# A gated linear recurrence in a decoder trunk: score products of two heads in one run, 64-column levels, later start of the head pairs

## The chip, the cores and the metric

One core of one Trainium2 chip runs the kernel. The metric is the device time of one execution in microseconds (us), as the median of several runs. TensorE (PE; PEld is its weight load) multiplies matrices, VectorE (DVE) and ScalarE (ACT) work element by element, GpSimd (POOL) and SyncE (SP) issue most of the transfers.

## What is computed

Two layers of a decoder trunk on 256 tokens of width 2048, all in float32. Layer 0 mixes tokens with a gated MLP (mixer A) and a gated linear recurrence with 8 heads of width 128 (mixer B), layer 1 with a forgetting attention; each layer ends with a gated MLP. The part that the change touches is mixer B:

```python
def hgrn2(q, f_logit, i, g, lower_bound, o_gain):
    ...
    log_f = jnp.logaddexp(jnp.log(lb), jnp.log1p(-lb) + jax.nn.log_sigmoid(fl))
    k = (1.0 - lb) * jax.nn.sigmoid(-fl)
    ...
    def step(state, xs):
        q_c, k_c, v_c, lf_c = xs
        G = jnp.cumsum(lf_c, axis=2)
        o_inter = jnp.einsum('bhtk,bhkv->bhtv', q_c * jnp.exp(G), state)
        diff = G[:, :, :, None, :] - G[:, :, None, :, :]
        decay = jnp.exp(jnp.where(mask[:, :, None], diff, -jnp.inf))
        scores = jnp.einsum('bhtk,bhtsk,bhsk->bhts', q_c, decay, k_c)
        o_intra = jnp.einsum('bhts,bhsv->bhtv', scores, v_c)
        ...
    o = rms_norm(o, o_gain) * jax.nn.silu(g.astype(f32).reshape(shp))
```

## The kernel before

The weights stream through the core once, and nearly all of TensorE's work is their products. A float32 weight tile w is split into two rounded halves: ScalarE writes wh (L212), VectorE the remainder wl = w - wh (L217), and three matmuls (wh with the high part of the activations, wl with the high part, wh with the low part) stand for one in full precision: L273 to L275 in project_tok, L293 to L295 in project_four. One call of weights() loads 128x1024 numbers into one of four buffers w; wh and wl have three buffers each. The 12 matmuls that use one such tile are called a step below; a projection to 512 columns has 8 steps.

Small work is fitted between the steps by generators. At each step tick() runs every generator in `free` and `flight` up to its next yield; `after(n, g)` starts one n ticks later; `depth[0]` limits how many taken from `queue` are in flight. The helpers behind(), act_in(), mm_in() and others (L150 to L168) fix where an instruction stands in its engine's queue: behind the last conversion, subtraction or weight matmul that was handed over. So the order on every engine is fixed when the program is built, and each engine works through its queue in that order; a wait holds everything behind it on the same engine.

In mixer_ab the projections run in the order w_v, then for j = 0, 1 w_f, w_q and w_i (gates, queries and values of four heads each), then w_u and w_g, and the output projection w_abo. queries(j) starts the heads: `after((4, 3)[j] * i + 1 - i // 2, hgrn(4 * j + i))`. hgrn(h) replaces the decay between tokens of 128 by products on seven levels (blocks of 64, 32, ... 1 tokens):

- Factors of keys and queries are scaled level by level on VectorE (L621 to L628) and copied by ScalarE into E (L617), which has two buffers.
- TensorE forms the product between the two halves of the sequence (from t, called kq in the profile, into a bank px) and two products of 64x64 for each level into the two banks `level` (levels in the profile): four levels in the first, three in the second, each 128 columns wide. For the first level the products lie off the diagonal blocks, for the others on them; the columns that no product writes were set to zero once (L430).
- VectorE masks each bank (L646) into smk and adds the seven levels one by one to st[:, 1] (L651), which was set to the diagonal before (L605). st has three buffers.
- Three yields later st[:, 1] is transposed on TensorE (L168), copied back by ScalarE (L658), and three products with the values itok give the output (px<-itok). Then follow the norm (two squares L669, rsq(), two scalings L673).

`finish`, `values` and `mixes` prepare mixer A; `of_queries` reads the query sums z once and sums into dgc (L702). gated(j) multiplies the gate of w_g into itok (zg, L720) and transposes it (L313). spatial(j) waits until all heads have ended, then takes a Gelu of w_u's result (turn) and splits eight blocks into ya, one block each second tick. Switching between function sets costs a table load on ScalarE (L97).

Of the kernel before, what the change touches and what calls it, by code (L numbers as in the profile page):

```python
# [15 lines left out]
P = 128  # L16
S = 256
# [18 lines left out]
LANE = 64  # L36
LEVELS = (64, 32, 16, 8, 4, 2, 1)
# [18 lines left out]
def tile_trunk(ctx: ExitStack, tc: tile.TileContext, x, pp_d, cst_d, mlev_d, msk_d,  # L56
# [367 lines left out]
    def mixer_ab(norm):  # L424
# [4 lines left out]
        for b in level:  # L429
            V.memset(b, 0.0)  # L430
# [54 lines left out]
        msk = hp.tile([P, NL * P], BF16, tag="msk", name="msk")  # L485
# [5 lines left out]
        def values():  # L491
            behind(V.tensor_copy(msk, kst), "sub")
# [103 lines left out]
        depth[0] = 3  # L596

        itoks, left = [], [NH]

        def hgrn(h):  # L600
# [32 lines left out]
            smk = hp.tile([P, NL * P], F32, tag="smk", name=nm("smk"), bufs=1)  # L633
            xps = bank()
            mm_in(xps[:, 0:P], t[:, 0], t[:, 1], start=True, stop=True)
            s128 = hp.tile([P, P], F32, tag="s128", name=nm("s128"), bufs=3)
            SC.activation(s128, xps[:, 0:P], AF.Copy)
            for c0, c1 in ((0, 4), (4, NL)):
                sps = level[c0 // 4]
                for li in range(c0, c1):  # L640
                    for g in range(2):
                        k0 = g * (P // 2)
                        q0 = P // 2 - k0 if li == 0 else k0
                        mm_in(sps[k0:k0 + P // 2, (li - c0) * P + q0:(li - c0) * P + q0 + P // 2],
                              E[:, li, 0, k0:k0 + P // 2], E[:, li, 1, q0:q0 + P // 2], start=True, stop=True)
                V.tensor_tensor(smk[:, c0 * P:c1 * P], sps[:, 0:(c1 - c0) * P],  # L646
                                msk[:, c0 * P:c1 * P], ALU.mult)
                for li in range(c0, c1):
                    n = LEVELS[li]
                    sv = view(st[:, 1], 0, (2 * n, 64 // n), (n - P, 2), (1, n))  # L650
                    V.tensor_tensor(sv, sv, smk[:, li * P:(li + 1) * P].rearrange(  # L651
                        "p (b two n) -> p b two n", two=2, n=n), ALU.add)
# [5 lines left out]
            SC.activation(st[:, 1], op[:, S:S + P], AF.Copy)  # L658
# [6 lines left out]
            PE.matmul(op[:, P:S], s128, i0, start=True, stop=False)  # L665
            PE.matmul(op[:, P:S], st[:, 1], i1, start=False, stop=True)
# [71 lines left out]
        def spatial(j, z):  # L738
            while left[0] or j and yB[4 * j - 1] is None:
                yield  # L740
            yield
            act_in(z, z, AF.Gelu)
            yield
            for i in range(4):
                b = 4 * j + i
                m = mg[b].rearrange("p (t n) -> p t n", t=2)
                sum_in(m, m, natural(z[:, i]), ALU.mult)
                yB[b] = quad("ya")
                split(yB[b], mg[b], turn=True)
                yield  # L750
                yield
# [480 lines left out]
```

## Time and profile before

| | us |
|---|---|
| median of 3 runs | 2286.31 |
| lowest and highest run | 2285.83, 2288.68 |
| profiled execution, its time | 2286.77 |
| profiled execution, span from first to last instruction | 2284.7 |
| granted TensorE clock, mean | 1.000 |
| of the span, TensorE busy | 2279.6 |
| VectorE busy | 1561.6 |
| ScalarE busy | 1312.6 |

How to read the rows: in a timeline a row is start, duration, engine, line, operation, output<-inputs, shapes and count, and in brackets how long the engine had been idle before it and what ended that. In the list of groups a row ends with the count, then busy us and the mean ns of one, then the idle time before. In the list of waits a row says who waited for whom: us in total, how many times, the longest. A float32 matmul leaves two records, one of the rounded form leaves one; matmuls overlap, so the distance between two starts, not the duration, is what one takes from TensorE.

### The profile page before, as it was taken

The numbers are of one execution on the slowest core, as the hardware profiler recorded it, in microseconds if no ns is written. First come the engines' busy times: TensorE is split into PE (matmuls) and PEld (weight loads), VectorE is DVE, ScalarE is ACT, GpSimd is POOL, SyncE is SP. The second block draws the span as 40 slices with busy tenths as digits, with TensorE's granted clock in tenths as the row PEclk, the third lists the DMA queues.
The fourth block names the chain that finished last, engine by engine and source line by source line (L and its number), as shares of the span: only waits on it lengthen the run. The fifth ranks groups of instructions, "written<-read, shape, count | busy, mean of one in ns | idle before, by whom it ended". The sixth has DMA issues, their size and how long they took to land. (4 is left out here: it accounts for less than half of the span.)

```text
span 2284.7 us, 31585 instructions
## 1 busy us (share of the span) xinstructions
PE 2279.6 (100%) x10486; PEld 1895.7 (83%) x10486; DVE 1561.6 (68%) x2378; ACT 1312.6 (57%) x1957; POOL 420.3 (18%) x779
## 2 busy tenths in 40 slices
PE   9999999999999999999999999999999999999999
PEld 8888888888888888888888888888888888888887
DVE  7888767767467657766775665667776466667766
ACT  7577756656456445554555556655665455455642
POOL 0212232221012002201322211322311012012102
PEclk9999999999999999999999999999999999999999
DMA  8756677777667667766676656677777667666765
GB/s 283 216 178 188 199 217 218 242 222 216 201 195 234 207 201 218 214 214 183 186 226 210 197 176 196 206 225 240 224 218 217 195 209 219 207 210 211 223 204 175
DMA packets 487908, 481.06 MB, mean 211 GB/s; under 512 B 102880, under 2 KB 454640, under 8 KB 487744
## 3 DMA queue, kind: packets, MB, share of 16 engines
q1 hardware_dynamic: 460080, 448.42, 63.6%
q0 software_dynamic: 25360, 27.37, 5.0%
q10 hardware_dynamic: 2304, 3.26, 0.4%
q8 instruction: 82, 1.34, 0.2%
q14 instruction: 82, 0.67, 0.1%
HBM read 434.85 MB, written 2.12 MB: 191 GB/s over the span
## 5 line engine op out<-in xcount | busy, mean ns | idle before, releaser
L217 DVE TENSOR_TENSOR wl<-w,wh 128x1024 fp32r<-128x1024 f32 (+1 forms) x814 | 987.2, 1216 | 632.3 <-ACT wh L212 622.3
L212 ACT ACTIVATE wh<-w 128x1024 fp32r<-128x1024 f32 (+1 forms) x814 | 854.6, 1052 | 779.5 <-PE pm L295 566.1
L293 PE MATMUL pm<-wh,a 128*128 128x512 f32 x1792 | 700.8, 391 | 0.0
L295 PE MATMUL pm<-wh,a 128*128 128x512 f32 x1792 | 698.1, 390 | 0.0
L294 PE MATMUL pm<-wl,a 128*128 128x512 f32 x1792 | 697.8, 389 | 0.0
L319 POOL DMA_DIRECT2D zt<-tmp x413 | 223.6, 549 | 1197.4 <-DVE tmp L313 1050.8
L295 PEld LDWEIGHTS pm<-wh,a 128*128 128x128 f32 x1792 | 336.5, 188 | 70.0
L293 PEld LDWEIGHTS pm<-wh,a 128*128 128x128 f32 x1792 | 336.6, 188 | 69.7
L294 PEld LDWEIGHTS pm<-wl,a 128*128 128x128 f32 x1792 | 336.6, 188 | 69.1
L319 POOL DMA_DIRECT2D turn<-tmp x336 | 182.0, 550 | 543.6 <-DVE tmp L313 314.0
L293 PE MATMUL pm<-wh,hid 128*128 128x512 f32 x688 | 267.9, 389 | 0.0
L294 PE MATMUL pm<-wl,hid 128*128 128x512 f32 x688 | 267.9, 389 | 0.0
L295 PE MATMUL pm<-wh,hid 128*128 128x512 f32 x688 | 267.8, 389 | 0.0
L273 PE MATMUL pm<-wh,a 128*128 128x512 f32 x456 | 181.0, 397 | 0.0
L274 PE MATMUL pm<-wl,a 128*128 128x512 f32 x456 | 178.0, 390 | 0.2 <-DVE wl L217 0.2
L275 PE MATMUL pm<-wh,a 128*128 128x512 f32 x456 | 177.9, 390 | 0.0
L293 PEld LDWEIGHTS pm<-wh,hid 128*128 128x128 f32 x688 | 129.2, 188 | 26.8
L294 PEld LDWEIGHTS pm<-wl,hid 128*128 128x128 f32 x688 | 129.2, 188 | 26.7
L295 PEld LDWEIGHTS pm<-wh,hid 128*128 128x128 f32 x688 | 129.2, 188 | 26.7
L313 DVE STREAM_TRANSPOSE tmp<-z 128x512 f32<-128x512 f32 x132 | 91.9, 705 | 20.2 <-ACT z L1008 18.7
L159 ACT ACTIVATE conv<-zt,pp 128x256 f32<-128x256 f32 x176 | 95.3, 589 | 14.4 <-DMA zt<-tmp 9.4
L274 PEld LDWEIGHTS pm<-wl,a 128*128 128x128 f32 x456 | 85.8, 188 | 17.9 <-DVE wl L217 0.9
(225 smaller groups left out, 1925.6 us busy)
## 6 DMA issues: line engine op xcount, KB each, us to landing
w<-in_w_up SPq DMA_DIRECT2D x352, 512.0 KB, 4.5
w<-in_w_dn SPq DMA_DIRECT2D x176, 512.0 KB, 4.5
w<-in_w_cqkv SPq DMA_DIRECT2D x88, 512.0 KB, 4.3
w<-in_w_abo SPq DMA_DIRECT2D x32, 512.0 KB, 4.4
w<-in_w_cg SPq DMA_DIRECT2D x32, 512.0 KB, 3.9
w<-in_w_co SPq DMA_DIRECT2D x32, 512.0 KB, 4.9
zt<-tmp SPq DMA_DIRECT2D x414, 32.0 KB, 2.5
zt<-tmp POOLq DMA_DIRECT2D x413, 32.0 KB, 2.5
```

The costliest lines, as they stand in the source:

```text
L159: return behind(SC.activation(*args, **kw), "act")
L212: deep["act"] = SC.activation(wh[:, p], w[:, p], AF.Copy)
L217: deep["sub"] = V.tensor_tensor(wl[:, p], w[:, p], wh[:, p].bitcast(F32), ALU.subtract)
L273: PE.matmul(ps[T], ah, h, start=k + i == 0, stop=False)
L274: PE.matmul(ps[T], ah, l, start=False, stop=False)
L275: deep["main"] = PE.matmul(ps[T], al, h, start=False, stop=k + i == KT - 1)
L293: PE.matmul(ps[T], ah, h, start=k + i == 0, stop=False)
L294: PE.matmul(ps[T], ah, l, start=False, stop=False)
L295: deep["mm"] = deep["main"] = PE.matmul(ps[T], al, h, start=False, stop=k + i == n - 1)
L313: V.transpose(tmp.rearrange("p (b m i t) -> p b m i t", b=4, m=4, t=2)[:, :, :, :, T], src(T).rearrange("p (m b j) -> p b m j", m=4, b=4))
L319: qs[(a + b) % len(qs)].dma_start(dst[BLK * b:BLK * (b + 1), :, a * n:(a + 1) * n], tmp[BLK * a:BLK * (a + 1), b * 4 * n:(b + 1) * 4 * n] ...
```

## The change

Four things are changed, all in mixer_ab.

- One run for two heads. The even head of a pair waits until the odd head's factors E are made, and issues the products of both: two kq products into one bank, then 14 level products of the even head and 14 of the odd one. The bank level[i] now holds all seven levels of one head, 64 columns each.
- Masking and adding. The first level is copied by ScalarE straight into its off-diagonal place in st (two copies of 64x64). The other six are multiplied with a mask of 384 columns by one instruction, summed by one reduction over the levels, multiplied with tri (which puts the sum into the two halves of the rows), and added with the diagonal piece dg by two instructions of 64 partitions.
- Score tiles are four fixed tiles sts, cleared once; the transposed scores go to s128[:, 1] instead of back into st. The masks tri and eye are made once in values(), which has two yields more.
- Times. START gives new starts for the heads (before: 1, 5, 8, 12 and 1, 4, 6, 9 ticks; now 1, 4, 11, 14 and 1, 3, 8, 10), depth[0] is 4 instead of 3, and spatial() yields twice only after every second block.

```diff
+HP = P // 2
+START = ((1, 4, 12, 15), (1, 3, 9, 11))
...
-        for b in level:
-            V.memset(b, 0.0)
...
-        msk = hp.tile([P, NL * P], BF16, tag="msk", name="msk")
+        msk = hp.tile([P, NL - 1, HP], BF16, tag="msk", name="msk")
+        tri = hp.tile([P, 2, HP], F32, tag="tri", name="tri")
+        eye = hp.tile([P, HP], F32, tag="eye", name="eye")
+        sts = [hp.tile([P, 2, P], F32, tag=f"st{i}", name=f"st{i}") for i in range(4)]
...
         def values():
-            behind(V.tensor_copy(msk, kst), "sub")
+            full = kst.rearrange("p (l c) -> p l c", l=NL)
+            for g in range(2):
+                k = slice(g * HP, (g + 1) * HP)
+                behind(V.tensor_copy(msk[k], full[k, 1:, k]), "sub")
+            sum_in(eye, ident[:, 0:HP], ident[:, HP:P], ALU.add)
+            yield
+            behind(V.memset(tri, 0.0), "sub")
+            for li in range(1, NL):
+                n = LEVELS[li]
+                part = view(tri[:, 1], 0, (2 * n, 32 // n), (n - HP, 2), (1, n))
+                V.tensor_tensor(part, part, msk[:, li - 1].rearrange("p (b two n) -> p b two n", two=2, n=n), ALU.add)
+            yield
+            for st in sts:
+                behind(V.memset(st, 0.0), "sub")
             yield
...
-        depth[0] = 3
+        depth[0] = 4
...
-            st = hp.tile([P, 2, P], F32, tag="st", name=nm("st"), bufs=3)
-            V.tensor_tensor(st, ident.unsqueeze(1).to_broadcast([P, 2, P]),
-                            dgc[:, h].unsqueeze(2).to_broadcast([P, 2, P]), ALU.mult)
+            st = sts[h % 4]
+            dg = hp.tile([P, 2, HP], F32, tag="dg", name=nm("dg"), bufs=4)
+            V.tensor_tensor(dg, eye.unsqueeze(1).to_broadcast([P, 2, HP]),
+                            dgc[:, h].unsqueeze(2).to_broadcast([P, 2, HP]), ALU.mult)
...
-            smk = hp.tile([P, NL * P], F32, tag="smk", name=nm("smk"), bufs=1)
-            xps = bank()
-            mm_in(xps[:, 0:P], t[:, 0], t[:, 1], start=True, stop=True)
-            s128 = hp.tile([P, P], F32, tag="s128", name=nm("s128"), bufs=3)
-            SC.activation(s128, xps[:, 0:P], AF.Copy)
-            for c0, c1 in ((0, 4), (4, NL)):
-                sps = level[c0 // 4]
-                for li in range(c0, c1):
-                    for g in range(2):
-                        k0 = g * (P // 2)
-                        q0 = P // 2 - k0 if li == 0 else k0
-                        mm_in(sps[k0:k0 + P // 2, (li - c0) * P + q0:(li - c0) * P + q0 + P // 2],
-                              E[:, li, 0, k0:k0 + P // 2], E[:, li, 1, q0:q0 + P // 2], start=True, stop=True)
-                V.tensor_tensor(smk[:, c0 * P:c1 * P], sps[:, 0:(c1 - c0) * P],
-                                msk[:, c0 * P:c1 * P], ALU.mult)
-                for li in range(c0, c1):
-                    n = LEVELS[li]
-                    sv = view(st[:, 1], 0, (2 * n, 64 // n), (n - P, 2), (1, n))
-                    V.tensor_tensor(sv, sv, smk[:, li * P:(li + 1) * P].rearrange(
-                        "p (b two n) -> p b two n", two=2, n=n), ALU.add)
+            made[h] = t, E
+            if h % 2 == 0:
+                while h + 1 not in made:
+                    yield
+                yield
+                xps = bank()
+                for i in range(2):
+                    ti = made[h + i][0]
+                    r = mm_in(xps[:, i * P:(i + 1) * P], ti[:, 0], ti[:, 1], start=True, stop=True)
...
+                for i in range(2):
+                    Ei = made[h + i][1]
+                    for li in range(NL):
+                        for g in range(2):
+                            k, q0 = slice(g * HP, (g + 1) * HP), (g if li else 1 - g) * HP
+                            r = mm_in(level[i][k, li * HP:(li + 1) * HP], Ei[:, li, 0, k],
+                                      Ei[:, li, 1, q0:q0 + HP], start=True, stop=True)
...
+                crossed[h] = crossed[h + 1] = xps
+            while h not in crossed:
+                yield
+            i = h % 2
+            s128 = hp.tile([P, 2, P], F32, tag="s128", name=nm("s128"), bufs=2)
+            SC.activation(s128[:, 0], crossed[h][:, i * P:(i + 1) * P], AF.Copy)
+            if i:
+                yield
+            for g in range(2):
+                k = slice(g * HP, (g + 1) * HP)
+                SC.activation(st[k, g, HP - g * HP:P - g * HP], level[i][k, 0:HP], AF.Copy)
+            smk = hp.tile([P, NL - 1, HP], F32, tag="smk", name=nm("smk"), bufs=1)
+            V.tensor_tensor(smk, level[i][:, HP:NL * HP].rearrange("p (l c) -> p l c", l=NL - 1), msk, ALU.mult)
+            own = hp.tile([P, HP], F32, tag="own", name=nm("own"))
+            V.tensor_reduce(own, smk.rearrange("p l c -> p c l"), AX.X, ALU.add)
+            both = smk[:, 0:2]
+            V.tensor_tensor(both, own.unsqueeze(1).to_broadcast([P, 2, HP]), tri, ALU.mult)
+            for g in range(2):
+                k = slice(g * HP, (g + 1) * HP)
+                V.tensor_tensor(st[k, :, k], both[k], dg[k], ALU.add)
...
-                after((4, 3)[j] * i + 1 - i // 2, hgrn(4 * j + i))
+                after(START[j][i] - i // 2, hgrn(4 * j + i))
...
                 split(yB[b], mg[b], turn=True)
                 yield
-                yield
+                if i % 2:
+                    yield
```

More of the change, by code (lines that the diff above doesn't have):

```diff
@@ L595, in mixer_ab @@
         yB = [None] * KT
-        depth[0] = 3
+        depth[0] = 4
         itoks, left = [], [NH]
+        made, crossed = {}, {}
         def hgrn(h):
@@ new lines, in hgrn @@
+            made[h] = t, E
[8 more added lines that the diff above has]
+                    if i:
+                        tc.add_manual_dep(r.ins, last.ins.name, order, reason="one run")
+                    last = r
+                for i in range(2):
[5 more added lines that the diff above has]
+                                      Ei[:, li, 1, q0:q0 + HP], start=True, stop=True)
+                            if not (li or g):
+                                tc.add_manual_dep(r.ins, last.ins.name, order, reason="one run")
+                    last = r
+                crossed[h] = crossed[h + 1] = xps
@@ L657, in hgrn @@
             turn_in(op[:, S:S + P], st[:, 1], ident)
-            SC.activation(st[:, 1], op[:, S:S + P], AF.Copy)
+            SC.activation(s128[:, 1], op[:, S:S + P], AF.Copy)
             yield
@@ L664, in hgrn @@
             mm_in(op[:, 0:P], st[:, 0], i0, start=True, stop=True)
-            PE.matmul(op[:, P:S], s128, i0, start=True, stop=False)
-            PE.matmul(op[:, P:S], st[:, 1], i1, start=False, stop=True)
+            PE.matmul(op[:, P:S], s128[:, 0], i0, start=True, stop=False)
+            PE.matmul(op[:, P:S], s128[:, 1], i1, start=False, stop=True)
             so = hp.tile([P, LANE], F32, tag="so", name=nm("so"), bufs=2)[:, 0:2]
```

1 line of the change is left out of this document (added).

## The prediction

> **What bounds the kernel now.** First the page: busy times by engine, then the chain that ended last.
>
> ```profile
> PE 2279.6 (100%) x10486; PEld 1895.7 (83%) x10486; DVE 1561.6 (68%) x2378; ACT 1312.6 (57%) x1957; POOL 420.3 (18%) x779
> PE 34%; DMA 1%; ACT 0%; issue 0%; POOL 0%; DVE 0%; ACTq 0%
> ```
>
> TensorE is busy throughout, and what the chain shows of other engines is 1%. Then the list of waits, TensorE's own part: whether it ever starves.
>
> ```profile
> PE pm L294 <- DVE wl L217: 0.3, 1, 0.3
> PE pm L274 <- DVE wl L217: 0.2, 1, 0.2
> ```
>
> Apart from the start, these two are all of it, 0.5 us in 2284.7. So time can come only from work taken off TensorE's own queue, and time is lost wherever a copy that TensorE needs comes late. Next the timeline of TensorE at one head of the recurrence, and the group of its small products.
>
> ```profile
> 125.73 0.39 PE L295 MATMUL pm<-wh,a 128*128 128x512 f32 x1
> ...
> 129.81 0.39 PE L295 MATMUL pm<-wh,a 128*128 128x512 f32 x1
> ...
> 142.52 0.38 PE L165 MATMUL px<-itok,st 128*128 128x128 f32 x2
> ...
> 143.18 0.39 PE L165 MATMUL px<-kq 128*128 128x128 f32 x2
> 143.50 1.03 PE L165 MATMUL levels<-E 128*64 128x64 f32 x28
> 144.47 0.50 PE L293 MATMUL pm<-wh,a 128*128 128x512 f32 x1
> 144.80 0.40 PE L294 MATMUL pm<-wl,a 128*128 128x512 f32 x1
> ```
>
> ```profile
> L165 PE MATMUL levels<-E 128*64 128x64 f32 x224 | 8.3, 226 | 0.0
> ```
>
> From 125.73 to 129.81 lie 18 weight matmuls: 0.227 us each, so a step of 12 takes 2.72 us. The three products with itok take 0.66 us (142.52 to 143.18), six records of 0.11. The product with kq takes 0.22 if its like follows it, but 0.32 ahead of the level products; and the first two matmuls behind these are 0.33 apart where 0.23 is usual. Going over to the 64-column form and back therefore costs something of its own.
>
> **The change part by part. One run for two heads.** From the start of the kq product to the second weight matmul, 143.18 to 144.80, are 1.62 us, less one matmul of 0.23: 1.39 for a head alone, or 1.17 without the kq product's 0.22. The 28 records start within 1.03 less one duration of 0.22, 0.81 for 27 steps: 0.030 each. A second head in the same run thus costs 28 x 0.030 = 0.84 instead of 1.17. Four pairs save 4 x 0.33 = 1.3 us. That is on the path in full, since TensorE never rests here. No product is dropped: the counts of all matmuls are equal. Putting a transposition behind the itok products instead of between weight matmuls I take at nothing, by the 0.11 us records above, which follow each other without a gap.
>
> **Masking and adding.** Rows of the groups of instructions:
>
> ```profile
> L651 DVE TENSOR_TENSOR st<-st,smk 128x128 f32<-128x128 f32 x56 | 16.9, 303 | 0.2
> ...
> L646 DVE TENSOR_TENSOR smk<-levels,msk 128x512 f32<-128x512 f32 (+1 forms) x16 | 9.4, 618 | 2.0 <-PE levels L165 2.0
> ...
> L501 DVE TENSOR_REDUCE ss<-junk 128x4 f32<-128x512 f32 x4 | 2.7, 686 | 0.1
> ```
>
> Removed per head on VectorE: seven adds of 0.30 and two masks of 0.62, 3.4 us. Added: one mask of 384 columns and one reduction over 384 elements (0.5 us each by three quarters of the rows of 512 columns), one product, one diagonal piece of half the old size and two adds of 64 partitions (0.3 each by the 128-element row), 2.2 us; the old 256-element diagonal goes too. No row shows a reduction that reads with a stride, or an add of 64 partitions: from half these prices to twice them. ScalarE gets two 64x64 copies a head, at most the 0.26 us of the 128x128 ones. All this saves VectorE some 10 us, and I cost it at nothing: the cover is the weight matmuls, for no wait of TensorE ends on these tiles. At twice the price some 13 us come back on eight heads, still under cover except where a weight's remainder (wl, L217) stands behind them; I allow 0.8 us for that. The one-time masks and the cleared st tiles (under 20 instructions) lie early, under the same cover.
>
> **Pairs begin later: two places in the queues.** START, the depth of 4 and the dropped yield in spatial() move heads against weight steps. The built order of both kernels on ScalarE and VectorE shows what follows from it. Before, ScalarE converts weights (L212) as far ahead as three buffers allow. Timeline of ScalarE, second query projection into the second i projection:
>
> ```profile
> 152.96 1.06 ACT L212 ACTIVATE wh<-w 128x1024 fp32r<-128x1024 f32 x1 [0.90 <-PE pm L295]
> ...
> 157.11 0.26 ACT L669 ACTIVATE itok<-px 128x128 f32<-128x128 f32 x1
> ...
> 158.58 0.20 ACT L101 ACTIVATE so<-rm 128x2 f32<-128x2 f32 x1 [0.30 <-DVE rm L350]
> ...
> 159.03 1.28 ACT L97 ACT_TABLE_LOAD   x1
> 160.33 0.63 ACT L673 ACTIVATE itok<-px,so 128x128 f32<-128x128 f32 x2
> 160.84 0.43 ACT L101 ACTIVATE lf<-turn 128x256 f32<-128x256 f32 x1
> 161.18 0.50 ACT L617 ACTIVATE E<-kq 128x128 f32<-128x128 f32 x2
> 161.57 0.42 ACT L101 ACTIVATE kq<-turn 128x256 f32<-128x256 f32 x1
> ...
> 165.70 1.06 ACT L212 ACTIVATE wh<-w 128x1024 fp32r<-128x1024 f32 x1
> ...
> 166.82 1.05 ACT L212 ACTIVATE wh<-w 128x1024 fp32r<-128x1024 f32 x1
> ...
> 168.26 0.68 ACT L565 ACTIVATE z<-pm,Rt 128x512 f32<-128x512 f32 x1
> 168.83 0.60 ACT L603 ACTIVATE lf<-lf,gm 128x256 f32<-128x256 f32 x1
> ```
>
> Here the weights of the first two i steps are converted (165.70, 166.82) before the query sums are taken out (z). VectorE keeps the same order:
>
> ```profile
> 166.79 2.36 DVE L217 TENSOR_TENSOR wl<-w,wh 128x1024 fp32r<-128x1024 f32 x2 [1.34 <-ACT wh L212]
> 169.07 0.29 DVE L702 SCALAR_TENSOR_TENSOR kt<-kt,z 128x128 f32<-128x128 f32 x1
> ...
> 169.92 0.71 DVE L313 STREAM_TRANSPOSE tmp<-z 128x512 f32<-128x512 f32 x1
> 170.55 0.25 DVE L702 SCALAR_TENSOR_TENSOR kt<-kt,z 128x128 f32<-128x128 f32 x1
> ...
> 267.97 0.69 DVE L720 TENSOR_TENSOR zg<-zg,itok 128x512 f32<-128x512 f32 x1
> ```
>
> In the changed order both z copies stand ahead of the second i step's conversion, and all eight L702 and both transpositions ahead of its wl. Let p be the end of head 1's itok products; 36 weight matmuls follow, so that step is wanted at p + 8.16. Its predecessor's conversion takes its buffer when those products begin, p - 0.66. ScalarE then has, in order: that conversion 0.96 (254.00 to 254.96 in the next fence), two L673 0.51, two squares, two E copies and the wait for rm 1.47 (157.11 to 158.58), Ln and Exp 0.45, a table load 1.30, two L673 0.51, four gates at 0.34 (160.84 to 161.18), 1.36, and two z at 0.57, 1.14: 7.70, so z is there at p + 7.04. VectorE then owes four L702 0.85 (169.07 to 169.92), two transpositions at 0.63 (169.92 to 170.55), two products at 0.2 (half the L702 pace of four in 0.85) and wl 1.18 (half of 2.36): 3.69, ready at p + 10.7. TensorE wants wl one matmul behind the start, p + 8.39. Late by 2.3 us; 1.8 if the 0.30 wait and a product pair drop out, 2.8 if z or rm wait longer.
>
> The second place is the first step of the second gate projection. ScalarE's rows of before:
>
> ```profile
> 253.06 1.06 ACT L101 ACTIVATE turn<-turn 128x1024 f32<-128x1024 f32 x1
> 254.00 1.05 ACT L212 ACTIVATE wh<-w 128x1024 fp32r<-128x1024 f32 x1
> 254.96 0.42 ACT L327 ACTIVATE ya<-mg 128x256 fp32r<-128x256 f32 x1
> ...
> 262.73 1.06 ACT L212 ACTIVATE wh<-w 128x1024 fp32r<-128x1024 f32 x1 [1.34 <-issue]
> ...
> 265.75 1.04 ACT L212 ACTIVATE wh<-w 128x1024 fp32r<-128x1024 f32 x1
> 266.76 0.69 ACT L101 ACTIVATE zg<-pm,Rt 128x512 f32<-128x512 f32 x1
> ```
>
> Before, the last head ends 15 steps ahead of the output projection, the Gelu of spatial(0) (253.06) and its four splits are spread over weight steps, and two conversions (262.73, 265.75) precede zg. In the changed order the last head ends 11 steps ahead, 36 matmuls ahead of this place: wanted at p' + 8.16, p' being the end of its itok products. Between lie squares to Ln 1.47, Ln and Exp 0.45, table 1.30, two L673 0.51, Gelu 0.94, table 1.30, two splits 0.68 (two of the 0.34 gates' form) and zg 0.57: 7.22. VectorE puts zg's product 0.69, a transposition 0.63 and wl 1.18 behind it: p' + 9.7, late by 1.3 against p' + 8.39. The squares don't start at p', however: head 6's norm, 12 matmuls earlier, and one conversion (0.96) are ahead in the queue, which puts them 0.5 to 1.1 later. Together 1.8 to 2.4; I take 2.1. The conversion itself is late by less and is inside both figures.
>
> On the table load the trace has 1.28 us with the next instruction 0.02 behind it (159.03, 160.33). [...]
>
> **Sum**, against the profiled execution's own 2286.77 us (its span is 2284.7): -1.3 + 2.3 + 2.1 = +3.1 us, 2289.9. That execution lies 0.46 us above the median of the runs, 2286.31. Predicted median: 2289.4 us, 0.14% slower. TensorE makes nothing good later, as it has no idle time from there on. The changed order of ya and yb in the output projection I take at nothing, since the splits have steps to spare (-0.3 to +0.5).
>
> **The rivals.** *The run pays and nothing starves:* wh and wl come in time because VectorE is 10 us lighter. 2286.3 - 1.3 = 2285.0 us. For it: TensorE hardly waits anywhere now. Against: the queue sums are made of copies and norms, not of the adds that fall away. Chance 0.16.
>
> *A run waits for its second head:* the joint products stand in TensorE's queue behind both heads' factors, and weight matmuls behind them can't pass. If the later head's last E copy comes after TensorE arrives, every microsecond late is one lost, in up to four runs. For it: both heads' decay chains share one VectorE; against: 24 or more matmuls of slack are put in by START. At 0.5 us a run, or 2 us at one: 2289.4 + 2.0 = 2291.4. It is decided where the second head's E lands later than the kq products' turn. Chance 0.14.
>
> *The new operations cost twice my price* and make wl late at a third place, like the first: 2289.4 + 2.3 + 0.8 = 2292.5. For it: no row shows them; against: a reduction costs no more per element than a product there (686 ns for 512). Chance 0.06.
>
> **How the numbers follow.** The forecast has 0.64. Its own range is 2288.1 to 2290.7: 1.8 + 1.8 - 1.3 = +2.3, less the 0.5 by which the lowest run of before lies under the median, and 2.8 + 2.4 - 1.3 + 0.5 = +4.4. With the first rival below and most of the second above, the range is 2285.0 to 2291.8. A measurement of this kernel can't tell 0.2%, 4.6 us, from no change: 2281.7 to 2290.9. Inside lie the first rival, but for 0.02 that I give to runs lower still, and the forecast, but for 0.05 at its upper edge; above lie that edge and the other two rivals. Faster 0.02, same 0.73, slower 0.25.
>
> **What would show it.** Per pair, 56 level records in one stretch of about 1.9 us and one return to 0.23; TensorE's waits should list two places near 170 and 268 us, at L273/L274's and L293/L294's successors, each with wl as releaser and together about 4.4 us. If TensorE's list stays as empty as now, the queue sums are wrong; if waits stand at the kq or level products, the second rival holds. VectorE's busy time should fall by 8 to 14 us without effect. An end below 2285.0 or above 2291.8 would mean a part I haven't seen.

## The result, and the profile after the change

| | before | after |
|---|---|---|
| median of 16 runs each, us | 2286.39 | 2292.32 |
| lowest and highest run, us | 2285.68, 2288.68 | 2291.08, 2294.35 |
| profiled execution, time, us | 2286.77 | 2291.73 |
| its span, us | 2284.7 | 2290.0 |

The ratio is 1.0024, with a 95% interval of 1.0017 to 1.0031; the medians differ by 5.9 us. The forecast was 2289.4, and its range ended at 2291.8, 0.5 us below the measured median. The direction was right, the size was not. The mean granted TensorE clock of the 16 runs after the change is 0.999 in eight of them, with a median of 2293.5 us, and 1.000 in the other eight, with a median of 2291.4.

Line numbers stand a little later in the changed kernel: the conversions are L214 (wh) and L219 (wl), the matmuls L275 to L277 (project_tok) and L295 to L297 (project_four), the small products L167, the E copies L635, the copies of the sums z L581, the sums into dgc L742, the transpositions on VectorE L315. First the page of the changed kernel: busy times by engine, and the engines' shares of the chain.

```profile
PE 2280.9 (100%) x10486; PEld 1895.3 (83%) x10486; DVE 1558.0 (68%) x2357; ACT 1313.7 (57%) x1971; POOL 421.3 (18%) x779
...
PE 96%; DVE 2%; DMA 1%; ACT 1%; issue 0%; SPq 0%; POOL 0%; ACTq 0%; DVEq 0%
```

TensorE is busy for 1.3 us more, although its instructions are equal in number, and the span is 5.3 us longer: most of the loss is waiting. Next the list of TensorE's waits, its four rows of weight matmuls.

```profile
PE pm L276 <- DVE wl L219: 1.2, 1, 1.2
PE pm L296 <- DVE wl L219: 1.1, 2, 0.9
...
PE pm L295 <- ACT wh L214: 1.0, 1, 1.0
PE pm L275 <- ACT wh L214: 1.0, 1, 1.0
```

Before, two rows with 0.5 us stood there. Now there are 4.3 us, 2.0 of them on ScalarE's part of a conversion. The timeline of TensorE shows the first place, the second step of the second i projection.

```profile
168.95 0.39 PE L277 MATMUL pm<-wh,a 128*128 128x512 f32 x1
170.33 0.73 PE L275 MATMUL pm<-wh,a 128*128 128x512 f32 x2 [0.99 <-ACT wh L214]
172.31 0.50 PE L276 MATMUL pm<-wl,a 128*128 128x512 f32 x1 [1.25 <-DVE wl L219]
172.64 0.39 PE L277 MATMUL pm<-wh,a 128*128 128x512 f32 x1
172.87 0.47 PE L275 MATMUL pm<-wh,a 128*128 128x512 f32 x1
...
176.99 0.40 PE L275 MATMUL pm<-wh,a 128*128 128x512 f32 x1
```

From 168.95 to 172.87 are five matmuls, 3.92 us where 5 x 0.227 would do: 2.8 us lost in the two waits. What follows was not foreseen at all. From 172.87 to 176.99 are eleven matmuls in 4.12 us, 0.43 apart for most of the way: another 1.6 us lost while TensorE waits for nobody. The table of stretches shows what it is; its columns are the length, the busy time of PE, PEld, DVE, ACT and POOL with their counts, then the granted clock, the DMA share and GB/s.

```profile
168.00:173.00 5.00, 2.77 (x11) 1.67 (x11) 5.00 (x25) 5.00 (x12) 1.68 (x3) 1.00 0.10 20
173.00:174.00 1.00, 1.00 (x5) 0.72 (x4) 1.00 (x2) 0.98 (x4) 1.00 (x3) 0.52 0.48 103
...
176.00:177.00 1.00, 1.00 (x5) 0.75 (x5) 0.46 (x3) 0.58 (x1) 1.00 (x3) 0.77 1.05 359
177.00:180.00 3.00, 3.00 (x15) 2.46 (x14) 2.32 (x7) 2.65 (x5) 0.91 (x2) 1.00 0.98 313
```

TensorE was granted half its clock for 3.41 us, from 173.04 to 176.46 (it is 0.61 in the stretch from 173.0 to 173.2 and 0.86 from 176.4 to 176.6). Over the whole span that is 0.999 instead of 1.000; where it was, only a table by stretches shows. The runs with 0.999 above have a median 2.1 us over that of the others, which fits this, but where in those runs the clock fell is not recorded. The second place, the first step of the second gate projection, loses 3.62 - 5 x 0.227 = 2.5 us between 270.22 and 273.84, and keeps its clock.

```profile
270.22 0.39 PE L297 MATMUL pm<-wh,a 128*128 128x512 f32 x1
271.63 0.73 PE L295 MATMUL pm<-wh,a 128*128 128x512 f32 x2 [1.03 <-ACT wh L214]
273.27 0.50 PE L296 MATMUL pm<-wl,a 128*128 128x512 f32 x1 [0.91 <-DVE wl L219]
273.61 0.39 PE L297 MATMUL pm<-wh,a 128*128 128x512 f32 x1
273.84 0.40 PE L295 MATMUL pm<-wh,a 128*128 128x512 f32 x1
```

Behind the matmuls at 294.71, 300.73 and 317.28 three more wl come late, in the output projection. From the first of these matmuls to its third successor:

```profile
294.71 0.39 PE L295 MATMUL pm<-wh,ya 128*128 128x512 f32 x1
295.34 0.50 PE L296 MATMUL pm<-wl,ya 128*128 128x512 f32 x1 [0.24 <-DVE wl L219]
...
295.93 0.40 PE L295 MATMUL pm<-wh,ya 128*128 128x512 f32 x1
```

1.22 - 3 x 0.227 = 0.5 us; the other two, read in the same way, cost 0.2 and 0.4, all three 1.1. The gain is there too: the joined products of a pair.

```profile
143.25 0.60 PE L167 MATMUL px<-kq 128*128 128x128 f32 x4
143.79 1.85 PE L167 MATMUL levels<-E 128*64 128x64 f32 x56
145.57 0.50 PE L295 MATMUL pm<-wh,a 128*128 128x512 f32 x1
145.91 0.40 PE L296 MATMUL pm<-wl,a 128*128 128x512 f32 x1
```

143.25 to 145.91, less one matmul, is 2.43 us for two heads; two heads alone take 2 x 1.39. Each of the four pairs saves 0.35 us, 1.4 in all.

Two marks on TensorE's timeline are used for the account, in every kernel below: the first product of the output projection (pm<-wh,ya), behind the recurrence, and the first of the feed-forward stage that follows.

| start of, us | output projection | feed-forward |
|---|---|---|
| before | 289.70 | 376.74 |
| after | 294.71 (+5.0) | 382.99 (+6.3) |

-1.4 + 2.8 + 1.6 + 2.5 is +5.5 at the first mark. The profiled execution was 0.4 ahead from its start on (its 181st weight matmul begins at 47.09, not 47.48), so 5.1 is what the rows explain of 5.0. The output projection adds 1.1 of 1.2. At the end of the span the distance is 5.3: before lost 0.55 us each to a late wl at 1126 and one at 1496 us (the two rows of its list of waits), and this execution did not. These lie in stages that the change does not touch, and the kernels below list waits of 0 to 2.1 us between 1090 and 1140 us.

### The profile page after: what moved, and what is told of

The parts are those of the page before. It is cut to its first block, busy times and chain, and to the rows that moved or that the text cites. A ratio compares the mean times of both kernels' runs of the same rounds, so it can differ in the third digit from the quotient of the medians.

```text
span 2290.0 us, 31600 instructions
## 1 busy us (share of the span) xinstructions
PE 2280.9 (100%) x10486; PEld 1895.3 (83%) x10486; DVE 1558.0 (68%) x2357; ACT 1313.7 (57%) x1971; POOL 421.3 (18%) x779
## 4 chain that ended last, share of the span: by engine, by line
PE 96%; DVE 2%; DMA 1%; ACT 1%; issue 0%; SPq 0%; POOL 0%; ACTq 0%; DVEq 0%
PE pm L295 26%; PE pm L297 26%; PE pm L296 26%; PE pm L276 5%; PE pm L275 5%; PE pm L277 5%; PE px L167 1%; PE pm L266 1%; DVE wl L219 1%; PE px L833 1%; PE pm L834 0%; DMA turn<-tmp 0%; DMA w<-in_w_abo 0%; ACT wh L214 0%; PE px L170 0%
## 5 line engine op out<-in xcount | busy, mean ns | idle before, releaser
L219 DVE TENSOR_TENSOR wl<-w,wh 128x1024 fp32r<-128x1024 f32 (+1 forms) x814 | 986.2, 1215 | 632.0 <-ACT wh L214 622.2
L214 ACT ACTIVATE wh<-w 128x1024 fp32r<-128x1024 f32 (+1 forms) x814 | 854.0, 1052 | 769.5 <-PE pm L297 548.0
L295 PE MATMUL pm<-wh,a 128*128 128x512 f32 x1792 | 699.9, 391 | 1.0 <-ACT wh L214 1.0
L297 PE MATMUL pm<-wh,a 128*128 128x512 f32 x1792 | 697.5, 389 | 0.0
L295 PEld LDWEIGHTS pm<-wh,a 128*128 128x128 f32 x1792 | 336.3, 188 | 70.8 <-ACT wh L214 1.4
L297 PEld LDWEIGHTS pm<-wh,a 128*128 128x128 f32 x1792 | 336.3, 188 | 70.3
L295 PE MATMUL pm<-wh,hid 128*128 128x512 f32 x688 | 267.6, 389 | 0.0
L297 PE MATMUL pm<-wh,hid 128*128 128x512 f32 x688 | 267.6, 389 | 0.0
L275 PE MATMUL pm<-wh,a 128*128 128x512 f32 x456 | 181.4, 398 | 1.0 <-ACT wh L214 1.0
L277 PE MATMUL pm<-wh,a 128*128 128x512 f32 x456 | 178.4, 391 | 0.0
L297 PEld LDWEIGHTS pm<-wh,hid 128*128 128x128 f32 x688 | 129.1, 188 | 26.9
L295 PEld LDWEIGHTS pm<-wh,hid 128*128 128x128 f32 x688 | 129.1, 188 | 26.7
L315 DVE STREAM_TRANSPOSE tmp<-z 128x512 f32<-128x512 f32 x132 | 91.7, 704 | 20.9 <-ACT z L1049 18.8
```

The source lines that it names most:

```text
L214: deep["act"] = SC.activation(wh[:, p], w[:, p], AF.Copy)
L219: deep["sub"] = V.tensor_tensor(wl[:, p], w[:, p], wh[:, p].bitcast(F32), ALU.subtract)
L275: PE.matmul(ps[T], ah, h, start=k + i == 0, stop=False)
L277: deep["main"] = PE.matmul(ps[T], al, h, start=False, stop=k + i == KT - 1)
L295: PE.matmul(ps[T], ah, h, start=k + i == 0, stop=False)
L297: deep["mm"] = deep["main"] = PE.matmul(ps[T], al, h, start=False, stop=k + i == n - 1)
```

## The experiments

Theory: the joining puts two heads' copies, norms and decay work into one stretch of ScalarE's and VectorE's queues, and the weight conversions behind it come late. Rivals: the later starts alone do it; the new masks and sums do it. For the slow matmuls: TensorE's standing still halves its clock, or something else that ran at 173 us does. Shifts at the first mark are against before's 289.70.

**Times alone.** The kernel before with START, depth 4 and the shorter spatial().

```diff
+START = ((1, 4, 12, 15), (1, 3, 9, 11))
...
-        depth[0] = 3
+        depth[0] = 4
...
-                after((4, 3)[j] * i + 1 - i // 2, hgrn(4 * j + i))
+                after(START[j][i] - i // 2, hgrn(4 * j + i))
...
-                yield
+                if i % 2:
+                    yield
```

> The kernel before with the changed times alone: the new starts of the eight heads, four states in flight, one yield less in the spatial output for every second tile. Every head keeps its own products, the 128-column masks and the old sums. Theory (the joined pairs put the scalar and vector work of two heads into one stretch, ahead of a weight conversion): no wait for a converted weight near 170 and 268 us, and a time within 0.6 us of the kernel before. Rival (the later starts push the heads' work into the i and gate projections, whoever computes it): both waits are there, and the time is 4 to 6 us above the kernel before.

Measured: 2286.93 us against 2286.61 before, ratio 1.0002 (0.9993 to 1.0011). Of the list of TensorE's waits, the one of `warm` at the start; beside it stands one of 0.3 us in a stage that the change does not touch.

```profile
PE warm L173 <- DVE ones L88: 1.1, 1, 1.1
```

First mark 290.38 (+0.7). The later starts alone make no wait there, and the changed order of ya and yb none either. What the 0.7 us are is not shown: no wait stands in the list for them.

**Joined pairs with the starts of before.**

```diff
-START = ((1, 4, 12, 15), (1, 3, 9, 11))
+START = ((1, 5, 9, 13), (1, 4, 7, 10))
```

> The changed kernel with the starts of before, (1, 5, 9, 13) and (1, 4, 7, 10), all else as changed. Theory (joined pairs crowd ScalarE and VectorE wherever they begin): the first head of a pair still waits for its second, so the waits don't go, they move; one of 4 to 6 us near 175 us with a second of about 1.5 us behind it, the place near 268 us is free of waits, and the time is 4 to 8 us above the kernel before. Rival (the later starts alone cost the 5.9 us): no waits, and the saving of four pairs, about 1.4 us, is left: 1 to 2 us below the kernel before.

Measured: 2297.25 us against 2286.61, ratio 1.0044 (1.0032 to 1.0057): 10.6 us, more than the theory's 8. Its waits:

```profile
PE pm L275 <- ACT wh L214: 6.0, 1, 6.0
PE pm L276 <- DVE wl L219: 1.6, 3, 0.8
...
PE px L167 <- DVE kq L639: 0.8, 1, 0.8
```

The wait of 6.0 us ends at 176.20, and the matmuls behind it run at half clock, 0.43 us apart, until 184 us. The last row is one that the prediction had as a rival: a run that stands on TensorE before its second head's factors (kq) are done. So the later starts are the cure, not the cause: with the old ones the joining costs nearly twice as much.

**The pair taken apart.** The changed kernel with its masks, sums and starts, but each head's products in a run of their own.

```diff
-            made[h] = t, E
-            if h % 2 == 0:
-                while h + 1 not in made:
-                    yield
...
+            i = h % 2
+            xps = bank()
+            mm_in(xps[:, i * P:(i + 1) * P], t[:, 0], t[:, 1], start=True, stop=True)
+            for li in range(NL):
...
+            crossed[h] = xps
```

> The changed kernel with the pair taken apart: every head's products are a run of their own, issued as soon as the head is ready, and its score tile is read as soon as its own run ends. The starts, the 64-column levels, the masks and the sums are those of the changed kernel. Theory (the joining is what crowds): no wait of 0.5 us or more near 170 and 268 us, and a time between 1.3 us below and 0.5 us above the kernel before. Rival (the new masks, sums and copies are what makes the conversions late, joined or not): the waits near 170 and 268 us are there with 1 us or more each, and the time is 3 us or more above the kernel before.

Measured: 2286.52 us against 2286.69, ratio 0.9999 (0.9990 to 1.0008). TensorE's list has the wait of `warm` at the start alone:

```profile
PE warm L174 <- DVE one L90: 1.1, 1, 1.1
```

First mark 289.90 (+0.2). This is the changed kernel in everything but the joining (with the even head's wait for the odd one, which belongs to it), and all 5.9 us are gone. The rival of the new operations falls. The starts alone, and the starts with the new operations, make no wait at the two places, so the joining is the cause.

**The second place alone.** The last two heads of the second group two ticks earlier.

```diff
-START = ((1, 4, 12, 15), (1, 3, 9, 11))
+START = ((1, 4, 12, 15), (1, 3, 7, 9))
```

> The changed kernel with the last two heads of the second group started two ticks earlier: (1, 3, 7, 9) for (1, 3, 9, 11). Theory (each place costs what its own two waits cost): no wait of the second gate projection near 268 to 274 us, the two waits near 170 us as in the changed kernel, and a time 2.0 to 3.0 us below it. Rival (the work is only moved, and something behind it is late by as much): a new wait of 1 us or more between 230 and 300 us and less than 1 us gained.

Measured: 2290.46 us, ratio to before 1.0014 (1.0005 to 1.0023), 1.9 below the changed kernel where at least 2.0 was expected. The waits near 270 us are gone and those of the output projection with them, but there is a new one, at the pair's run:

```profile
240.30 0.39 PE L296 MATMUL pm<-wl,a 128*128 128x512 f32 x1
241.72 0.49 PE L167 MATMUL px<-kq 128*128 128x128 f32 x2 [1.02 <-DVE kq L639]
```

The second head was two ticks too early for VectorE: the new wait of 1 us is the rival's, the gain is not. First mark 292.25: 2.5 earlier than in the changed kernel; some 1.6 of that is the clock, which stayed at 1.00 behind the same two waits of the first place in this execution.

**The first place alone.** Later starts for heads 2 and 3 of the first group, and later gates for the second.

```diff
-START = ((1, 4, 12, 15), (1, 3, 9, 11))
+START = ((1, 4, 14, 17), (1, 3, 9, 11))
+GATE = (6, 8)
...
-            after(LAG, four_gates(j, turn(w_f[4 * j:4 * j + 4], use=of_keys(j))))
+            after(GATE[j], four_gates(j, turn(w_f[4 * j:4 * j + 4], use=of_keys(j))))
```

> As the kernel with the other times in this batch, but the second group's heads begin as in the changed kernel (1, 3, 9, 11): the first place alone is mended. Theory (the places are independent, and the first costs its waits and, in some executions, slow matmuls behind them): no waits near 170 us, all matmuls there 0.227 us apart, the waits near 268 us as in the changed kernel, and a time 2.5 to 4.7 us below the changed kernel's 2292.3. Rival (the places share one cause upstream, so that the second grows when the first goes): the second place's waits grow by 1 us or more, and less than 1.5 us is gained.

Measured: 2289.88 us, ratio to before 1.0013 (1.0004 to 1.0022), 2.4 below the changed kernel, a little under the theory. No wait of 0.3 us near 170 and no slow matmul; the second place as it was. But the first wl of the output projection is now 1.0 us late where it was 0.4:

```profile
291.81 0.50 PE L296 MATMUL pm<-wh,ya 128*128 128x512 f32 x1
293.07 0.50 PE L297 MATMUL pm<-wl,ya 128*128 128x512 f32 x1 [0.76 <-DVE wl L220]
```

With the run ahead of it: these waits are there when the second place is, and gone when the last pair begins earlier. They are the tail of the last pair's late end, not of the new order of ya and yb alone, which the times-alone kernel has without them. One of them, 0.5 us at 322.78, also stands in the kernel with the starts of before, which has no second place.

**Both places.** As above, with (1, 3, 8, 10) for the second group.

> The changed kernel with other times for three things: heads 2 and 3 of the first group begin at ticks 14 and 17 (12 and 15), heads 2 and 3 of the second group at 8 and 10 (9 and 11), and the gates of the second group wait 8 ticks (6). Theory (the joined pairs save 0.36 us each, and only the conversions that stand behind a pair's work took it back): the waits near 170 and 268 us and the slow matmuls behind the first are gone, no new wait is over 0.3 us, and the time is 1.0 to 2.2 us below the kernel before. Rival (the crowding has only moved, as when the heads began as before): a new pair of waits of 1 us or more somewhere between 140 and 330 us, and a time at or above the kernel before.

Measured: 2286.78 us against 2286.69, ratio 1.0000 (0.9991 to 1.0009). It is 5.5 us better than the change and not better than before; the theory's 1.0 us is not there. First mark 289.57 (-0.1). Some 0.9 of the 1.4 us saved were spent at a third crowd, a place where copies pile up: a wl at 194 us, and two waits of the itok products for the copied scores (s), near 197 and 201 us. From the timelines of TensorE and of its weight load, the first two:

```profile
194.13 0.48 PE L296 MATMUL pm<-wh,a 128*128 128x512 f32 x1
194.74 0.51 PE L297 MATMUL pm<-wl,a 128*128 128x512 f32 x1
...
197.39 0.30 PEld L168 LDWEIGHTS px<-itok,st 128*128 128x128 f32 x2 [0.29 <-ACT s L699]
```

**Whose crowd that is.** Two kernels: gates two ticks later still (10 for 8), and with that heads 2 and 3 one tick earlier (13, 16).

> The changed kernel with its first group's last two heads at ticks 14 and 17, the second group's at 8 and 10, and the gates of the second group 10 ticks late (8 in the run mended before it, which waited some 0.9 us between 194 and 202 us where those gates' work met the states of heads 2 and 3). Theory (that crowd is of the second group's gates and parts from the states when the gates come two ticks later): no wait of 0.3 us or more between 120 and 340 us, TensorE ahead of the kernel before by 0.8 to 1.6 us behind the last state, a time 0.5 to 1.7 us below the kernel before, which is about what can be told from it. Rival (what is saved is always paid at the next crowd): waits of 0.8 us or more in sum elsewhere between 140 and 300 us, TensorE ahead by less than 0.4 us there.

> As the run ahead of it, with heads 2 and 3 of the first group one tick earlier, at 13 and 16. Theory and rival as there; if the first place is what decides, its waits of up to 1 us come back near 170 us and the time is 0.5 to 1.5 us above the run ahead of it.

Measured, the first: 2287.16 us against 2286.50, ratio 1.0000 (0.9991 to 1.0009); the same waits at 194 to 201 us, first mark 289.67 (0.0). The gates are not what crowds there; the theory was wrong, and the rival held. The second: no wait at 170, 0.1 us at 194, and the first mark at 288.84, 0.9 ahead of before, the only kernel of this list that keeps more than half of the pairs' 1.4 us. Its time shows nothing of it: 2288.09 us, ratio 1.0005 (0.9996 to 1.0014). Its profiled execution waited 1.4 us for two late wl between 1090 and 1140 us, in the stage named above. No kernel was measurably faster than the one before, and with 1.4 us to win none could have been: the intervals reach some 2 us to either side.

**The clock, by itself.** The kernel before with ScalarE copies put ahead of one weight conversion at 18 places of the last feed-forward stage, far behind the recurrence.

```diff
+DOSES = (10, 12, 14, 16, 18, 20)
+PLACES = {18 + 13 * i: DOSES[i % 6] for i in range(18)}
...
+                if late["n"] in PLACES:
+                    prev = deep["act"]
+                    for _ in range(PLACES[late["n"]]):
+                        d = SC.activation(scr, scr, AF.Copy)
...
             deep["act"] = SC.activation(wh[:, p], w[:, p], AF.Copy)
```

> The kernel before with 10, 12, 14, 16, 18 or 20 added ScalarE copies of 128x256 ahead of one weight conversion at 18 places of the last feed-forward stage, each size three times, so that TensorE waits there for wh and then for wl, for various lengths (about 0 to 4 us); no recurrence is near. Theory (TensorE is granted half its clock for about 3 us once it has stood still for some 2 us within 3 us, whatever it waited for): matmuls behind the waits of over about 2 us in sum come 0.43 us apart for 3 us, at a granted clock near 0.5, and such a place loses 1.5 to 2 us more than its waits; behind shorter ones they come 0.227 us apart. Rival (the slow matmuls at 173 to 176 us of the changed kernel come from what else ran there, its transfers or the copies that share the banks): the clock stays at 1.00 behind all the waits made here, and each place loses its waits alone.

> The probe again with more copies: 17, 19, 21, 23, 25 or 27 ahead of one conversion at the 18 places, which makes waits of about 1 to 8 us. Theory (TensorE's clock is halved when it stands still for most of a window of some 3.4 us, whose start has nothing to do with the work): no slow matmuls behind waits of under 2.3 us in sum, some behind 2.3 to 3.2 us by chance, and about 3 us of matmuls 0.43 us apart behind nearly all of more than that, 8 of them each time however long the wait was. Rival (the halving goes on in proportion to the wait): the number of slow matmuls grows with the wait; a wait of 5 us and more is followed by twice as many as one of 3 us.

Measured, the first: 2297.40 us. Most of its copies fitted into ScalarE's slack: for the 18 places the list has four waits for wh, 4.1 us in all. Of the waits, a pair of 1.79 and 0.52 us (from 1893 us) was followed by eight matmuls 0.43 apart; one of 1.27 and 0.53 us was not. With no recurrence near, the rival falls. The second (2337.0 us) made 16 places with waits. Two of them, from the timeline of TensorE:

```profile
1764.20 0.39 PE L310 MATMUL pm<-wh,hid 128*128 128x512 f32 x1
1766.62 0.74 PE L308 MATMUL pm<-wh,hid 128*128 128x512 f32 x2 [2.03 <-ACT wh L225]
1767.88 0.50 PE L309 MATMUL pm<-wl,hid 128*128 128x512 f32 x1 [0.53 <-DVE wl L232]
...
1800.64 0.39 PE L310 MATMUL pm<-wh,hid 128*128 128x512 f32 x1
1802.20 0.73 PE L308 MATMUL pm<-wh,hid 128*128 128x512 f32 x2 [1.17 <-ACT wh L225]
1803.45 0.64 PE L309 MATMUL pm<-wl,hid 128*128 128x512 f32 x1 [0.52 <-DVE wl L232]
1803.90 0.63 PE L310 MATMUL pm<-wh,hid 128*128 128x512 f32 x1
```

Behind the longer waits (2.03 and 0.53) the clock is 1.00 from 1768 to 1771 us; behind the shorter ones (1.17 and 0.52) it is 0.50 from 1804 to 1807. So the length alone does not decide, against my lower bound of 2.3 us. The five slow stretches, ended where the distance goes back from 0.43 to 0.23, end near 1691.0, 1807.1, 1919.7, 2148.4 and 2226.9 us. Their distances are 34, 33, 67 and 23 times 3.413 us. The same time stands in the first execution of the changed kernel: its half clock at 173.04 us lasts 3.41 us, and the clock falls to half again behind the last matmul, at 2289.30 (0.65 in the stretch from 2289 to 2290), 620 times 3.4133 later. With that grid laid over the span of the second probe, and TensorE's idle time added up in each of its windows:

| window of 3.413 us | idle in it, us | next window |
|---|---|---|
| ends 1684.2 | 2.26 | half clock, and the one behind it |
| ends 1803.7 | 1.70 | half clock |
| ends 1916.3 | 2.68 | half clock |
| ends 2145.0 | 1.79 | half clock |
| ends 2220.1 | 3.41 | half clock, and the one behind it |
| ends 2216.7, 1766.1, 1612.5, 1725.2 | 1.58, 1.53, 1.54, 1.47 | full clock |

The waits at 1766 us were cut by a window's edge into 1.53 and 1.02. In these windows the half clock goes with TensorE's standing still for about half a window (1.70 us or more, against 1.58 or less), not with the length of a wait. The number of slow matmuls is 7 or 8, where 8 were expected, when one window was at half clock. Behind the waits of 3.12 and 5.55 us it is 10 for both, so it does not grow in proportion to the wait. There the clock stayed at half for two windows, as the stretches behind the longer one show:

```profile
2214.00:2222.00 8.00, 2.41 (x8) 1.15 (x6) 2.59 (x3) 7.72 (x15) 4.34 (x8) 0.88 0.64 172
2222.00:2226.00 4.00, 4.00 (x10) 3.14 (x11) 4.00 (x8) 1.48 (x3) 0.00 (x0) 0.50 0.67 214
2226.00:2229.00 3.00, 3.00 (x13) 2.44 (x12) 1.70 (x4) 1.71 (x3) 0.00 (x0) 0.85 0.82 261
```

That is 1.9 + 4 + 0.9 us, 6.8 in all. The first of the two windows at half clock still had 0.6 us idle in it (0.9 at 1684 us), and the next one was at half too; a window at full clock with 1.02 us idle (it ends at 1769.5) was followed by full clock. In the kernel with the starts of before it is three windows, to 184.0 us, with 2.5 and 0.75 us idle in the first two. At 0.2 us each, 7 to 10 slow matmuls cost a place 1.4 to 2.0 us.

**The changed kernel, twice more.**

> The changed kernel itself, looked at once more. Theory (the clock's window starts anywhere): the two waits near 170 us are there again with 1.1 and 1.4 us within 0.05; the slow matmuls behind them may be there or not, and without them TensorE is some 1.6 to 2.0 us earlier at 200 us than in the first look. Rival (they belong to the kernel): eight matmuls 0.43 us apart from 173 to 176 us again.

> The changed kernel once more, as the run ahead of it: the same two waits; the slow matmuls there or not (theory), or there again (rival).

Measured: 2293.07 and 2292.19 us, with the two waits at 170 us alike in both (2.8 us lost). The slow matmuls are there in the first of the two and not in the second. The stretch from 173 to 174 us in the one and in the other:

```profile
173.00:174.00 1.00, 1.00 (x4) 0.78 (x3) 1.00 (x3) 0.98 (x4) 1.00 (x3) 0.62 0.46 102
```

```profile
173.00:174.00 1.00, 1.00 (x5) 0.81 (x5) 1.00 (x4) 1.00 (x3) 1.00 (x2) 1.00 0.53 111
```

First marks 294.79 and 293.52. With the kernel of the second place, whose first place is unchanged, that is half clock in two profiled executions of four. The grid of windows fits the three of the changed kernel. In the first two executions of the changed kernel the half clock begins at 173.04 and 173.24, and the window that ends there has 1.94 and 1.85 us idle. In the third the clock falls to half only behind the last matmul, at 2290.84 (0.92 in the stretch from 2290 to 2291); the grid through that moment has an edge at 171.17, which parts the two waits into 0.98 and 1.25 us. So in these executions the half clock goes with where in a window the waits fall, and the 1.6 us are paid in some executions only. The mean clocks of all runs fit: 0.999 in eight of 16 of the changed kernel and in six of 11 of the kernel of the second place, whose six have a median 1.8 us above the other five, and in one of 55 of the five kernels without waits at either place (times alone, pair taken apart, both places, and the two with gates 10 ticks late). It is also 0.999 or less in four of 11 where the second place alone is left; those are no slower than the others, and why is open.

The feed-forward mark, which lies ahead of the stage near 1100 us, lies 6.3, 6.0 and 5.3 us behind before in the three executions.

## Why the prediction fell short

The measured median lies 0.5 us above the range's end. The forecast's own terms reached to 2290.7; the range went up to 2291.8 for a rival, a run that waits for its second head, which did not happen. So the eight runs at a mean clock of 1.000, with a median of 2291.4, are inside the range by luck. The terms one by one:

- **One run for two heads**, -1.3: right; 2.43 us for a pair, 1.4 us in all, on the path in full.
- **Masking and adding at nothing:** right in effect; the pair taken apart has all of it and no wait. The sizes were off: VectorE's busy time fell by 3.6 us, not 8 to 14. The reduction takes 0.84 us (priced 0.5), as a row of the groups of instructions shows, and the one-time masks and cleared tiles, in four groups, 3.4 us.

```profile
L687 DVE TENSOR_REDUCE own<-smk 128x64 f32<-128x384 f32 x8 | 6.7, 842 | 0.1
```

- **First place**, +2.3: right in place, conversion and cause; the size was 2.8, the upper end of what was allowed. The timelines of ScalarE and VectorE show what the queue sum lacked:

```profile
167.01 1.27 ACT L581 ACTIVATE z<-pm,Rt 128x512 f32<-128x512 f32 x2
168.15 0.53 ACT L635 ACTIVATE E<-kq 128x128 f32<-128x128 f32 x2
168.55 0.78 ACT L103 ACTIVATE lf<-turn 128x256 f32<-128x256 f32 x2
169.21 2.02 ACT L214 ACTIVATE wh<-w 128x1024 fp32r<-128x1024 f32 x2
```

```profile
169.44 1.30 DVE L315 STREAM_TRANSPOSE tmp<-z 128x512 f32<-128x512 f32 x2
...
171.03 1.22 DVE L219 TENSOR_TENSOR wl<-w,wh 128x1024 fp32r<-128x1024 f32 x1
```

Two E copies and two gates stood between z and the conversion, 1.06 us that the sum did not have. TensorE waited 1.0 us for wh itself and then 1.25 for wl, where the forecast had wl as the releaser and the conversion late by less. VectorE went through both transpositions and two products ahead of wl, as forecast. That the two places' rows in the list of waits add up to some 4.2 us, near the forecast 4.4, is luck: by the distances they cost 2.8 + 2.5 = 5.3.
- **Second place**, +2.1: measured 2.5, above the 2.4 that was allowed, again with wh late ahead of wl.
- **"The changed order of ya and yb ... at nothing":** the order alone does cost nothing, but behind the joined pairs the splits did not have steps to spare. The last pair's late end, which is the second place's cause, reaches into the output projection: 1.1 us of late wl in the first execution, 0.9 to 1.5 us between the two marks in the three. This term failed, and it was allowed 0.5 at most.
- **The sum itself** failed in what it left out: it charged a wait by its length. Behind the two waits of the first place the clock was at half for a window in two of three profiled executions, 1.6 us each. The profile of before could not show it, since no wait in it behind the start is over 0.3 us.
- **"TensorE makes nothing good later":** right, but for the late wl of other stages. From the feed-forward mark to the end of the span the three executions go from +6.3 to +5.3, from +6.0 to +6.6 and from +5.3 to +5.7.
- **The rivals:** that nothing starves did not happen. A run that waits for its second head did not happen in the changed kernel, but appears (1.0 and 0.8 us) when pairs begin earlier, so the two dangers pull in opposite directions. New operations at twice the price did not happen: the pair taken apart has them without a wait.

By terms: -1.4 + 2.8 + 2.5 + 1.1 is +5.0, and +6.6 where the clock is halved; forecast was +3.1, measured +5.9 between medians. Against the median of before, 2286.4, the eight runs at 1.000 lie at +5.0 and the eight at 0.999 at +7.1.

What stays open: which work makes the third crowd at 194 us when heads 2 and 3 begin at ticks 14 and 17 (one tick earlier removes it, later gates don't), what takes the rest of the saving there, and why conversions near 1100 us come late in some executions.

## What to carry to other kernels

Joining small products of two streams saves an engine's changes of form, here 0.35 us a pair, but it also lines up everything that leads to them and follows from them; on an engine that never rests, look at what that puts ahead of the next conversion before counting the gain. A list of moved work should be summed up to the conversion itself, with every copy between, and followed to the stage behind. And here waits on TensorE cost more than their length where they filled half a window of the clock together (1.70 of 3.41 us or more): those of 1.0 and 1.25 us lost 1.6 us more where most of both fell into one window than where an edge parted them.

## What the runs showed of the hardware

- In the second probe the half clock began and ended on a grid of 3.413 us. At full clock a window with 1.70 us idle was followed by half clock, one with 1.58 by full clock. At half clock a window with 0.6 to 0.9 us idle was followed by another at half, and one filled with work by full clock. In the three executions of the changed kernel, whose two waits at 170 us are alike, edges of such a grid lie at 173.04, 173.24 and 171.17 us.
- A reduction over a strided axis of 6, with 384 elements and 64 sums, took 842 ns (L687 after the change); one along the row, with 512 elements and 4 sums, took 686 (L501 before it). Whether the stride or the number of sums costs this is not shown.
